# One token-block order and one early weight split in a fused decoder block on one core

## The chip, the cores and the metric

The kernel runs on one core of a Trainium2 chip. The metric is the device time in microseconds (us) of one execution of the whole program. The engines are TensorE (PE; its weight loads are PEld), VectorE (DVE), ScalarE (ACT), GpSimd (POOL) and SyncE (SP), which issues every DMA of this kernel from one in-order queue.

## The reference, cut to what matters

One decoder layer over 1024 tokens of width 1024, all in float32: a hybrid token mixer (convolution, stick-breaking attention, RWKV-7), cross-attention into 256 memory tokens, and a gated feed-forward part with a convolution. Each begins with an RMS norm, each is added to the stream, and a final norm follows.

```python
def rms_norm(x, g):
    y = x * lax.rsqrt(jnp.mean(x * x, axis=-1, keepdims=True) + RMS_EPS)
    return y * g

def conv_ffn(hn, w_up, conv_w, conv_b, w_down):      # w_up 1024 x 5632, w_down 2816 x 1024
    u = causal_dwconv(hn @ w_up, conv_w) + conv_b     # width 3, per channel, along tokens
    gate, val = jnp.split(u, 2, axis=-1)
    return (jax.nn.silu(gate) * val) @ w_down

h = h + mix                                           # token mixer, projected by w_mix_out
h = h + memory_cross_attention(rms_norm(h, norm_ca), rms_norm(mem, norm_mem), ca_wq, ca_wkv, ca_wo)
h = h + conv_ffn(rms_norm(h, norm_ffn), ffn_up, ffn_conv_w, ffn_conv_b, ffn_down)
return rms_norm(h, norm_final)
```

## The kernel before, in words

**Numbers.** Every float32 operand of a large product is split into a rounded part "hi" and a rest "lo" (ACT casts hi, then VectorE or POOL computes source minus hi). A product is three matmuls per contraction block: hi·hi, hi·lo, lo·hi, each 128 x 128 by 128 x 512.

**Stages.** The token mixer ends with a merge: activations mh and ml (pool "ma") are multiplied with rows of w_mix_out (pool "wm") and accumulated into the eight token tiles h0 to h7 (128 tokens x 1024). `accumulate` (L1070) does such a sum: for each token tile, all matmuls into a two-bank PSUM tile (pool pd, two buffers), then one VectorE addition into h[i] (L1088), or an ACT copy (L1091) where there is nothing to add to, then a callback `after(i)`. Then comes cross-attention: `norm_T` (L193) normalises the eight tiles, transposes them on TensorE and splits them into hh and hn_lo; `q_proj` makes the queries of a head (L245 to L247 for head 0, by halves of 512 tokens), `attend` the head's output, and an `accumulate` with rows of ca_wo adds it to h.

**Into the feed-forward part.** The last of these accumulations (L1316) has the callback `operands(i)`, tile after tile in the order 0 to 7: store h[i] to h_d, normalise (sum of squares on ACT L189, short one-column operations on VectorE L190 and L176 to L181, the multiply by rs and the gain at L1277, written into h[i] or h[i−6]), transpose (L1296), copy back into h (L1299), and `put` split operands into X (L1280: ACT cast, lo on POOL for t1, t3 and t4, on VectorE otherwise).

The up product uses a two-by-two block scheme with seven products instead of eight. Blocks are the halves of the model width and the even or odd token tiles. b11 and b21 come from even tiles alone; b22, t1, t2, t3 and t4 need an even tile and the odd one behind it (L1305 to L1314).

**Up.** For each of 22 tiles f (L1370): four raw weight blocks are loaded, sums of weights are made on POOL (`wsum` L1332), each of seven weights is split (`parts` L1339, L1340), and seven products of twelve matmuls follow in the order b11, b21, t2, t3, t4, t1, b22 (L1346 to L1348); VectorE adds them up (L1368), then come the convolution (L1360 to L1364), the Silu, the product on POOL (L1399) and the store to hid_d[f].

**Down.** hid_d[0] and row 0 of ffn_down are loaded, split (`pair`) and multiplied without an addition; then groups of 2, 2, 3, 3, 3, 4, 4 rows follow. The first group has the callback `residual` (POOL adds h_d back, L1417), the last `final` (norm and store).

**Order.** The program is written in program order with priorities (`tc.high_priority`); a scheduler puts the instructions of each engine in order by priority and by when it expects operands to be ready. Each engine then runs in order.

**Memory.** Pools are stacks, from the left or (side right) from the right end of SBUF; the size of a pool is the sum of its tiles, and a tile that takes the place of a closed pool's tile waits for the last reader of that tile (`reuse_waits="tile"`). In bytes per partition: constants end at 2432; the mixer's pools mconst, wf, ft, mg and ma follow each other from there, ma from 59776 (four mh of 4096) with its four ml from 76160 to 92544. Cross-attention then opens, from 2432 again, wc (18432: weights of wq), can (19456: gain, junk, four ss, rs and rt each, two xs), and after can is closed wo (20480), co (16384), cq and ca. hn_lo (on the right) lies over wm.

Of the kernel before, what the change touches and what calls it, by code (L numbers as in the profile page):

```python
# [15 lines left out]
P = 128  # L16
# [30 lines left out]
POOL_T = ("t1", "t3", "t4")  # L47
AHEAD_TILES = 2
# [3 lines left out]
def hybrid_block(tc, A, out):  # L52
# [30 lines left out]
    with root:  # L83
# [100 lines left out]
        def rms(pl, xt, junk=None):  # L184
# [6 lines left out]
            return rsqrt(pl, ss, 1)  # L191
# [939 lines left out]

        with ExitStack() as st:
            wp = pool(st, "wc", 2)
            s3 = ExitStack()
            hnp = pool(s3, "hn", side=RIGHT)
# [7 lines left out]
            wo = pool(st, "wo", 2)  # L1143
            op = pool(st, "co", 2)
# [126 lines left out]
            gb = bcast_row(np_, A["norm_ffn"][0:1, :], "gb")  # L1271

            def normed(i):
# [14 lines left out]
            def operands(i):  # L1288


                with tc.high_priority(offset=100):
                    xs = normed(i)
                for b in range(2):
                    ps = PQ()
                    for j in range(4):
                        pe.transpose(out=ps[:, j * P:(j + 1) * P],  # L1296
                                     in_=xs[:, (4 * b + j) * P:(4 * b + j + 1) * P],
                                     identity=ident)
                    s_.copy(half(i, b), ps.rearrange("p (j t) -> p j t", j=4))  # L1299
# [15 lines left out]

            accumulate(wo, o, wrows, after=operands, rbufs=2)  # L1316

        with fst as st:
            up = A["ffn_up"][0].rearrange("(k p) c -> p k c", p=P)
            wp = pool(st, "wu")  # L1320
            wpt = [wp.tile([P, 2, 4, P], F32R, name="wp", bufs=10)]

            def raw(kh, c):
                t = wp.tile([P, 4, P], F32, name="raw", bufs=6)
# [155 lines left out]
```

## Time and profile before

| | us |
|---|---|
| median of three runs | 2319.57 |
| lowest and highest run | 2318.44, 2321.55 |
| profiled execution | 2328.44 |
| its span, first to last instruction | 2326.7 |
| TensorE busy in it | 2218.7 (95%) |
| VectorE, ACT, POOL busy | 1459.3, 896.5, 571.2 |

The profile is of one execution, which was 8.9 us longer than the median of the runs. All positions are us from the start of its span. Matmuls overlap: one of 512 columns shows about 0.39 us and the next starts earlier, so rates are read from the distance between starts. A few matmul records are missing in any stretch.

### The profile page before, as it was taken

What the parts mean: (1) busy time and instruction counts of PE and PEld (TensorE: products, weight loads), DVE (VectorE), ACT (ScalarE), POOL (GpSimd) and SP (SyncE); (2) the same over time, 40 slices, a digit from 0 to 9 for tenths busy, and PEclk for the clock granted to TensorE, in tenths of its full rate; (3) what the DMA queues carried; (4) which work ended last, traced back from release to release, by engine and by line L of the source; (5) the groups of instructions that cost most, each with busy time, mean ns of one, the idle gap of its engine ahead of it and who ended that gap; (6) DMA issues with size and microseconds to landing.
All of it is one profiled execution on the core that took longest, in us unless ns stands there. A gap on an engine that the chain in (4) does not pass through costs nothing.

```text
span 2326.7 us, 29997 instructions
## 1 busy us (share of the span) xinstructions
PE 2218.7 (95%) x11635; PEld 1838.7 (79%) x11635; DVE 1459.3 (63%) x1994; ACT 896.5 (39%) x1494; POOL 571.2 (25%) x489
## 2 busy tenths in 40 slices
PE   6999999999999999999998999996899999989998
PEld 5888878878888888887877878884788888867886
DVE  7576555672254254356767675449988888867535
ACT  6644233433344244345431153225444444442212
POOL 1124322232232233221112000002544444413000
PEclk9999989998999999999999999997899999999999
DMA  4334624433211211214767121103222222155311
GB/s 156 120 111 157 209 77 133 143 87 92 73 48 52 82 64 53 84 55 150 231 208 259 57 60 32 32 28 109 73 82 82 82 82 82 67 179 185 108 33 73
DMA packets 230112, 237.89 MB, mean 102 GB/s; under 512 B 35283, under 2 KB 188113, under 8 KB 228945
## 3 DMA queue, kind: packets, MB, share of 16 engines
q1 hardware_dynamic: 229969, 235.97, 31.3%
q8 instruction: 91, 1.49, 0.3%
q14 instruction: 52, 0.43, 0.1%
HBM read 169.87 MB, written 66.06 MB: 101 GB/s over the span
## 4 chain that ended last, share of the span: by engine, by line
PE 77%; DVE 12%; DMA 3%; issue 3%; ACT 3%; POOL 1%; SPq 0%; DVEq 0%; ACTq 0%; POOLq 0%
PE pd L276 6%; PE pd L275 6%; PE pd L279 6%; PE pd L1082 5%; PE pd L1083 5%; PE pd L1086 5%; PE pd L1346 3%; PE pd L1348 3%; PE pd L1347 3%; PE pd L257 3%; PE pd L260 3%; PE pd L256 3%; PE pq L1346 2%; PE pq L1348 2%; PE pq L1347 2%
## 5 line engine op out<-in xcount | busy, mean ns | idle before, releaser
L235 ACT CAST wh<-wr 128x512 fp32r<-128x512 f32 x270 | 159.0, 621 | 364.5 <-PE pd L1086 105.6
L236 POOL TENSOR_TENSOR wl<-wr,wh 128x512 fp32r<-128x512 f32 x128 | 177.4, 1403 | 261.1 <-ACT wh L235 247.7
L275 PE MATMUL pd<-xn_hi,wh 128*128 128x512 f32 x576 | 227.7, 395 | 0.0
L1088 DVE TENSOR_TENSOR h<-pd,h 128x1024 f32<-128x1024 f32 x120 | 146.5, 1221 | 126.8 <-PE pd L1086 126.5
L276 PE MATMUL pd<-xn_lo,wh 128*128 128x512 f32 x576 | 225.1, 391 | 0.0
L279 PE MATMUL pd<-xn_hi,wl 128*128 128x512 f32 x576 | 178.4, 391 | 0.0
L256 PE MATMUL pd<-xn_hi,wh 128*128 128x512 f32 x384 | 152.8, 398 | 0.0
L257 PE MATMUL pd<-xn_lo,wh 128*128 128x512 f32 x384 | 152.3, 397 | 0.0
L236 DVE TENSOR_TENSOR wl<-wr,wh 128x512 fp32r<-128x512 f32 x142 | 105.9, 768 | 60.8 <-ACT wh L235 60.5
L929 DVE TENSOR_TENSOR_SCAN B<-B 128x128 f32<-128x128 f32 (+3 forms) x64 | 87.0, 1359 | 85.1 <-POOL B L926 84.8
L279 PEld LDWEIGHTS pd<-xn_hi,wl 128*128 128x128 f32 x576 | 108.0, 188 | 23.6 <-POOL wl L236 0.2
L276 PEld LDWEIGHTS pd<-xn_lo,wh 128*128 128x128 f32 x576 | 108.4, 188 | 19.8
L275 PEld LDWEIGHTS pd<-xn_hi,wh 128*128 128x128 f32 x576 | 108.2, 188 | 19.5
L260 PE MATMUL pd<-xn_hi,wl 128*128 128x512 f32 x384 | 122.9, 398 | 0.0
L1340 DVE TENSOR_TENSOR wp<-ws,wp 128x512 fp32r<-128x512 f32 x88 | 121.0, 1375 | 2.4 <-ACT wp L1339 1.8
L1399 POOL TENSOR_TENSOR h<-h,h 128x1024 f32<-128x1024 f32 x22 | 52.8, 2402 | 227.5 <-DVE h L1364 192.7
L946 DVE TENSOR_TENSOR al<-pq,ah 128x512 fp32r<-128x512 f32 x80 | 54.6, 688 | 85.7 <-ACT ah L945 85.2
L1346 PE MATMUL pq<-t,wp 128*128 128x512 f32 x264 | 102.8, 389 | 2.5 <-ACT wp L1339 2.5
L1339 ACT CAST wp<-ws 128x512 fp32r<-128x512 f32 x88 | 54.7, 622 | 128.5 <-POOL ws L1332 66.0
L1347 PE MATMUL pq<-t,wp 128*128 128x512 f32 x264 | 102.9, 390 | 0.0
L1348 PE MATMUL pq<-t,wp 128*128 128x512 f32 x264 | 102.7, 389 | 0.0
L945 ACT CAST ah<-pq 128x512 fp32r<-128x512 f32 x80 | 46.9, 587 | 144.7 <-PE pq L941 144.4
(395 smaller groups left out, 5807.0 us busy)
## 6 DMA issues: line engine op xcount, KB each, us to landing
wr<-in_w_comb_dram SPq DMA_DIRECT2D x124, 256.0 KB
raw<-in_ffn_up_dram SPq DMA_DIRECT2D x88, 256.0 KB
gate_d<-ft SPq DMA_DIRECT2D x24, 512.0 KB
hid_d<-h SPq DMA_DIRECT2D x22, 512.0 KB
wr<-in_ffn_down_dram SPq DMA_DIRECT2D x42, 256.0 KB
t<-hid_d SPq DMA_DIRECT2D x21, 512.0 KB
wr<-in_ca_wkv_dram SPq DMA_DIRECT2D x32, 256.0 KB
ft<-gate_d SPq DMA_DIRECT2D x16, 512.0 KB
```

The source lines that it names most:

```text
L235: s_.copy(hi[:, sl], raw)
L236: (v_ if lo_e == "dve" else g_).tensor_tensor(lo[:, sl], raw, f32(hi[:, sl]), ALU.subtract)
L256: pe.matmul(o, wh(k), xh(k, h), start=k == 0, stop=False)
L257: pe.matmul(o, wh(k), xl(k, h), start=False, stop=False)
L260: pe.matmul(o, wl(k), xh(k, h), start=False, stop=k == nk - 1)
L275: pe.matmul(o, wh(k), xh(k, h), start=k == 0, stop=False)
L276: pe.matmul(o, wh(k), xl(k, h), start=False, stop=False)
L279: pe.matmul(o, wl(k), xh(k, h), start=False, stop=k == nk - 1)
L1088: v_.tensor_tensor(h[i], ps, h[i], ALU.add)
L1346: pe.matmul(ps, wh[:, k, :], xh[:, k, :], start=k == 0, stop=False)
L1347: pe.matmul(ps, wh[:, k, :], xl[:, k, :], start=False, stop=False)
L1348: pe.matmul(ps, wl[:, k, :], xh[:, k, :], start=False, stop=k == 3)
```

## The change

- The last attention accumulation takes the token tiles in the order 0, 2, 4, 6, 1, 3, 5, 7. Its callback `after` normalises tile i at once, and `operands` of an even tile follows once more than two tiles are waiting; odd ones come behind the accumulation.
- The weights of b11 and b21 for f = 0 and 1 are loaded and split ahead of this accumulation (`early_parts`, in a new pool "early"), and these four products stand between `operands` of the odd tiles.
- The normalised tile gets its own buffer xs (three) instead of a place in h. For even tiles POOL multiplies by the gain and ACT by rs; for odd ones VectorE does both, as before.
- `operands` reads the transposed tile from PSUM for splits and subtractions where it read a copy in h; odd tiles have only their first half copied.
- `rms` has its own short chain, with one VectorE operation less.
- wo and co are opened before wc, behind "early"; wc moves into the stack that closes with the queries.
- At f = 14, hid_d[0] and row 0 of ffn_down are loaded and split into the "early" tiles (`early_pair`), and the down part begins with them in the order 4, 0, 1, 5, 3, 7, 6, 2. The first group's two weight rows and activations go into the top tile by `pair`.

```diff
@@ rms
-            return rsqrt(pl, ss, 1)
+            r = pl.tile([P, 1], F32, name="rs", bufs=4)
+            t = pl.tile([P, 1], F32, name="rt", bufs=4)
+            s_.activation(t, ss, AF.Sqrt)
+            v_.reciprocal(r, t)
+            v_.scalar_tensor_tensor(t, r, ss, r, ALU.mult, ALU.mult)
+            v_.tensor_scalar(t, t, -0.5, 1.5, ALU.mult, ALU.add)
+            v_.tensor_tensor(r, r, t, ALU.mult)
+            return r
@@ cross-attention
+        est = ExitStack()
+        early = pool(est, "early")
         with ExitStack() as st:
-            wp = pool(st, "wc", 2)
+            wo = pool(st, "wo", 2)
+            op = pool(st, "co", 2)
             s3 = ExitStack()
+            wp = pool(s3, "wc", 2)
...
-            wo = pool(st, "wo", 2)
-            op = pool(st, "co", 2)
             ap = pool(s3, "cq", 2)
@@ into the feed-forward part
+            def early_parts(kh, c):
+                t = early.tile([P, 4, P], F32, name="er")
+                dma(t, up[:, 4 * kh:4 * kh + 4, c * P:(c + 1) * P])
+                w = early.tile([P, 2, 4, P], F32R, name="ew", bufs=4)
+                s_.copy(w[:, 0], t)
+                g_.tensor_tensor(w[:, 1], t, f32(w[:, 0]), ALU.subtract)
+                return w[:, 0], w[:, 1]
+
+            first = [[early_parts(kh, f) for kh in range(2)] for f in range(2)]
...
-                rs = rms(np_, h[i])
-                xs = h[i] if i < 6 else h[i - 6]
-                v_.scalar_tensor_tensor(xs, h[i], rs, gb, ALU.mult, ALU.mult)
+                xs = np_.tile([P, D], F32, name="xs", bufs=3)
+                if i % 2 == 0:
+                    g_.tensor_tensor(xs, h[i], gb, ALU.mult)
+                    s_.activation(xs, xs, AF.Copy, scale=rms(np_, h[i]))
+                else:
+                    v_.scalar_tensor_tensor(xs, h[i], rms(np_, h[i]), gb, ALU.mult, ALU.mult)
...
-            def operands(i):
+            def operands(i, xs):
                 q = i // 2
+                p1, p2 = turned(xs, 0), turned(xs, 1)
                 if i % 2 == 0:
-                    put("b11", half(i, 0), q)
-                    put("b21", half(i, 1), q)
+                    for b, (n, ps) in enumerate((("b11", p1), ("b21", p2))):
+                        put(n, ps, q)
+                        s_.copy(half(i, b), ps)
                     return
                 b11, b21, b12, b22 = half(i - 1, 0), half(i - 1, 1), half(i, 0), half(i, 1)
-                put("b22", b22, q)
+                s_.copy(b12, p1)
                 v_.tensor_tensor(b11, b12, b11, ALU.subtract)
                 put("t1", b11, q)
-                v_.tensor_tensor(b12, b22, b12, ALU.subtract)
+                v_.tensor_tensor(b12, p2, b12, ALU.subtract)
                 put("t3", b12, q)
-                v_.tensor_tensor(b22, b22, b11, ALU.subtract)
+                v_.tensor_tensor(b22, p2, b11, ALU.subtract)
+                put("b22", p2, q)
                 put("t2", b22, q)
...
-            accumulate(wo, o, wrows, after=operands, rbufs=2)
+            todo = []
+            def after(i):
+                with tc.high_priority(offset=100):
+                    todo.append((i, normed(i)))
+                if len(todo) > LAG and todo[0][0] % 2 == 0:
+                    operands(*todo.pop(0))
+            accumulate(wo, o, wrows, after=after, rbufs=2, order=(0, 2, 4, 6, 1, 3, 5, 7))
+            done = []
+            for f in range(2):
+                done.append(even_products(*first[f]))
+                for _ in range(1 + f):
+                    operands(*todo.pop(0))
+            operands(*todo.pop(0))
+            for f in range(2):
+                even_sums(f, *done[f])
@@ up
+                if f >= 2:
+                    even_sums(f, *even_products(parts(a11), parts(a12)))
...
+                if f == EARLY_DOWN:
+                    d0 = early_pair(hid_d[0]), early_pair(down[0])
@@ down
-            accumulate(None, [pair(d0, h[0], hid_d[0], "a")], [pair(d0, h[4], down[0], "w")],
-                       add=False, order=(2, 6, 0, 4, 1, 5, 3, 7))
...
+                if gi == 0:
+                    ws = [pair(None, hp2.tile([P, T], F32, name="t", bufs=3), down[k], x[1])
+                          for k, x in zip(ks, tiles[2:])]
+                    accumulate(None, [d0[0]], [d0[1]], add=False, order=(4, 0, 1, 5, 3, 7, 6, 2))
+                    gbf = bcast_row(hp2, A["norm_final"][None, :], "gbf")
+                    accumulate(None, acts, ws, after=residual)
```

`even_products` issues the products of b11 and b21 into one pd tile, `even_sums` copies and adds them; `early_pair` loads a row in two halves through the one er tile, casts on ACT and subtracts on POOL. LAG is 2, EARLY_DOWN is 14.

## Rows read from the trace of the kernel before

**Rows 1.** The page, engine totals: busy us, share of the span, instructions.
```profile
PE 2218.7 (95%) x11635; PEld 1838.7 (79%) x11635; DVE 1459.3 (63%) x1994; ACT 896.5 (39%) x1494; POOL 571.2 (25%) x489
```
**Rows 2.** Windows: us, busy us of each engine (instructions), granted clock, DMA share, GB/s.
```profile
1353.30:1385.10 31.80, 30.00 (x151) 23.47 (x152) 25.12 (x48) 14.61 (x27) 0.00 (x0) 1.00 0.30 88
1610.00:1620.00 10.00, 1.94 (x8) 1.57 (x8) 10.00 (x14) 5.56 (x12) 6.17 (x5) 0.50 0.08 32
1660.00:2060.00 400.00, 400.00 (x1750) 326.52 (x1750) 345.35 (x367) 167.01 (x225) 178.06 (x98) 1.00 0.25 80
```
**Rows 3.** Waits of TensorE, 1500 to 1660: who for whom, us, times, longest.
```profile
PE pq L1296 <- DVE h L1277: 12.6, 2, 7.6
PE pq L1296 <- DVE ss L190: 6.2, 2, 4.3
```
**Rows 4.** Waits of TensorE, 2040 to the end.
```profile
PE pd L1082 <- ACT h L1091: 3.5, 2, 2.8
PE pd L1082 <- DVE h L1088: 3.3, 2, 2.6
PE pd L1083 <- DVE wl L1429: 1.8, 1, 1.8
```
**Rows 5.** Timeline of TensorE, several stretches: start, us, line, operands, [idle before].
```profile
1384.86 0.39 PE L247 MATMUL pd<-top,wl 128*128 128x512 f32 x1
...
1574.43 0.73 PE L1082 MATMUL pd<-wh,oh 128*128 128x512 f32 x2 [1.92 <-ACT wh L235]
...
1637.36 0.40 PE L1348 MATMUL pd<-top,wp 128*128 128x512 f32 x1
1640.26 0.50 PE L1346 MATMUL pq<-t,wp 128*128 128x512 f32 x1 [2.50 <-ACT wp L1339]
...
2062.47 0.39 PE L1348 MATMUL pd<-b,wp 128*128 128x512 f32 x1
...
2063.15 0.39 PE L1348 MATMUL pd<-b,wp 128*128 128x512 f32 x1
...
2317.15 0.61 PE L1086 MATMUL pd<-wh,al 128*128 128x512 f32 x2
```
**Rows 6.** VectorE by line, 1577 to 1640: busy us, mean ns, idle before.
```profile
L1277 DVE SCALAR_TENSOR_TENSOR h<-h,rs,gb 128x1024 f32<-128x1024 f32 x8 | 13.8, 1740 | 0.0
L1088 DVE TENSOR_TENSOR h<-pd,h 128x1024 f32<-128x1024 f32 x8 | 9.7, 1218 | 3.6 <-PE pd L1086 3.5
...
L1311 DVE TENSOR_TENSOR h<-h,h 128x512 f32<-128x512 f32 x4 | 4.8, 1205 | 0.0
...
L178 DVE TENSOR_TENSOR rt<-rs 128x1 f32<-128x1 f32 x8 | 3.3, 426 | 0.0
...
L1309 DVE TENSOR_TENSOR h<-h 128x512 f32<-128x512 f32 x4 | 2.7, 681 | 0.2 <-ACT h L1299 0.2
L179 DVE TENSOR_TENSOR rt<-rt,ss 128x1 f32<-128x1 f32 x8 | 2.2, 290 | 0.0
```
**Rows 7.** The page's costliest groups: busy us, mean ns, idle before.
```profile
L236 POOL TENSOR_TENSOR wl<-wr,wh 128x512 fp32r<-128x512 f32 x128 | 177.4, 1403 | 261.1 <-ACT wh L235 247.7
...
L1340 DVE TENSOR_TENSOR wp<-ws,wp 128x512 fp32r<-128x512 f32 x88 | 121.0, 1375 | 2.4 <-ACT wp L1339 1.8
L1399 POOL TENSOR_TENSOR h<-h,h 128x1024 f32<-128x1024 f32 x22 | 52.8, 2402 | 227.5 <-DVE h L1364 192.7
```
**Rows 8.** Timeline of VectorE, cross-attention's norm.
```profile
1336.30 0.16 DVE L177 RECIPROCAL rs<-rt 128x1 f32<-128x1 f32 x1
...
1337.27 1.28 DVE L210 SCALAR_TENSOR_TENSOR xs<-h,rs,gb 128x1024 f32<-128x1024 f32 x1
...
1353.47 4.94 DVE L222 TENSOR_TENSOR hn_lo<-pq,top 128x512 fp32r<-128x512 f32 x8
...
1372.89 1.29 DVE L222 TENSOR_TENSOR hn_lo<-pq,top 128x512 fp32r<-128x512 f32 x2 [0.23 <-ACT top L221]
```
**Rows 9.** Timeline of ACT, the first Square of that norm.
```profile
1333.61 1.06 ACT L189 ACTIVATE junk<-h 128x1024 f32<-128x1024 f32 x1 [9.43 <-DVE h L1088]
```

More of the change, by code (lines that the diff above doesn't have):

```diff
@@ L1357, in q3, with plus, places, even_products @@
                 return ps.rearrange("p (q t) -> p q t", t=P)
+            def plus(o, ps, x):
+                v_.tensor_tensor(o, q3(ps), q3(x), ALU.add)
+            def places(f):
+                e = f % 2
+                return h[2 * e], h[4 + 2 * e], h[2 * e + 1], h[5 + 2 * e]
+            def even_products(w11, w12):
+                ab = PD()
+                return product(ab[:, 0:512], w11, "b11"), product(ab[:, 512:1024], w12, "b21")
+            def even_sums(f, pa, pb):
+                t0, t1, u0, u1 = places(f)
+                s_.copy(t0[:, 0:512], pa)
+                plus(blocks(u0)[0], pb, t0[:, 0:512])
@@ new lines, in hybrid_block, with early_pair, raw, wsum @@
+            operands(*todo.pop(0))
+            for f in range(2):
+                even_sums(f, *done[f])
+        with fst as st:
+            wp = pool(st, "wu")
+            down = [A["ffn_down"][0, k * P:(k + 1) * P, :] for k in range(NF)]
+            def early_pair(src):
+                ws = [early.tile([P, 2, 4, P], F32R, name="ew", bufs=4)
+                      .rearrange("p x a t -> p (x a t)") for _ in range(2)]
+                for sl in (slice(0, 512), slice(512, 1024)):
+                    t = early.tile([P, 4, P], F32, name="er").rearrange("p a t -> p (a t)")
+                    dma(t, src[:, sl])
+                    s_.copy(ws[0][:, sl], t)
+                    g_.tensor_tensor(ws[1][:, sl], t, f32(ws[0][:, sl]), ALU.subtract)
+                return ws
+            def raw(kh, c):
+                t = wp.tile([P, 4, P], F32, name="raw", bufs=6)
+                with tc.high_priority(offset=400):
+                    dma(t, up[:, 4 * kh:4 * kh + 4, c * P:(c + 1) * P])
+                return t
+            def wsum(x, y, op):
+                t = wp.tile([P, 4, P], F32, name="ws", bufs=3)
+                with tc.high_priority(offset=ahead):
+                    g_.tensor_tensor(t, x, y, op)
+                return t
+            def parts(src):
+                t = wp.tile([P, 2, 4, P], F32R, name="wp", bufs=10)
+                hi, lo = t[:, 0], t[:, 1]
+                with tc.high_priority(offset=ahead):
+                    s_.copy(hi, src)
+                    v_.tensor_tensor(lo, src, f32(hi), ALU.subtract)
+                return hi, lo
@@ L1365, in conv @@
                                         ALU.mult, ALU.add)
[L1367 to L1368 removed]
             for f in range(NF):
[L1371 removed]
                 ahead = 0 if f < AHEAD_TILES else 100
[L1373 removed]
+                t0, t1, u0, u1 = places(f)
                 (u0e, u0o), (u1e, u1o) = blocks(u0), blocks(u1)
@@ L1430, in pair, with hidden @@
                 return hi, lo
[L1432 to L1443 removed]
+            def hidden(ks, tiles):
+                return [pair(x[0], hp2.tile([P, T], F32, name="t", bufs=3), hid_d[k], x[1])
+                        for k, x in zip(ks, tiles)]
             f = 1
```

68 lines of the change are left out of this document (17 added, 51 removed).

## Prediction

> **What bounds the kernel now.** TensorE is busy for 95% of the span [rows 1], so only stretches in which it waits or runs slowly can be won. I read the page first, then ten-microsecond windows, then the waits of TensorE in the two thin stretches. The first lies where cross-attention hands over to the feed-forward part: in 1610 to 1620 TensorE is busy for 1.94 us of 10 while VectorE is full, and the granted clock is 0.50, the lower of its two levels [rows 2]. TensorE's transposes wait there for the normalisation on VectorE, 12.6 and 6.2 us [rows 3]. The second lies where the down products begin [rows 4].
>
> How much is there? A 512-column matmul comes every 0.227 us (three from 2062.47 to 2063.15 [rows 5]). From 1574.43, the start of the last attention accumulation, to 2063.38, the end of the up products, 489.0 us pass. They hold 96 + 1848 matmuls, 440.7 us, and 64 transposes, 7.7 us by an estimate of 0.12 each. So 40.6 us are lost. From 2063.38 to 2317.76, the end of the last matmul, 254.4 us hold 1056 matmuls, 239.4: 15.0 lost, of which 8.6 are the three waits of [rows 4]. No edit here can win more than about 55 us.
>
> **Into the feed-forward part: 18 us won.** VectorE sets this stretch. What the change takes from it, by [rows 6]: four of the eight normalising multiplies (even tiles go to POOL and ACT), half of 13.8, 6.9 us; the subtraction behind b22 now reads PSUM, so its four go from 1.205 to the 0.681 of the line above it that already did (4.8 to 2.7), 2.1; the two short operations of L178 and L179 become one, 5.5 less about 3.0, so 2.5. Together 11.5 us. The first matmul that needs odd tiles (product t2) then starts at 1640.26 − 11.5 = 1628.8 [rows 5]. By then TensorE has done 48 up matmuls instead of the 12 done now (one product, ended at 1637.8 [rows 5]), as both even tiles' products of f = 0 and 1 lie beside odd transposes: 36 × 0.227 = 8.2 us more. That cover costs TensorE nothing, since it idled there. Against it, VectorE needs 345.35 / 400 × 19.05 = 16.4 us per up tile [rows 2], and f = 0 and 1 now have only 60 matmuls, 13.6 us, for 16.4 − 2 × 1.375 [rows 7] = 13.7 us of it: I take 2 us of stall. 11.5 + 8.2 − 2 = 18 (17.7). The low end is 6.5, should the VectorE saving vanish; the high end 30, as most of 40.6 needs both operands and weights, which stay behind the last h_d stores in SP's queue. The four early weight loads are moved ahead of those eight stores; their ACT casts and POOL subtractions (4 × 1.40 by the POOL line of [rows 7]) lie before 1585, where POOL is empty; without that cover they would cost POOL 5.6 us.
>
> What is late next is POOL: four h·gb multiplies of 2.40 us (L1399's form [rows 7]) join it, with the odd tiles' t-parts queued behind them.
>
> *The port.* An operation of the kind of L1277 took 1.28 us with POOL idle [rows 8] and 1.74 on average here; L1088, with one input in PSUM, kept 1.218 [rows 6]. The Trainium skill, SBUF — State Buffer, "Who interferes with whom", says that a VectorE instruction with two SBUF inputs and a GpSimd one that reads SBUF lock each other out for a whole instruction. The rows agree. By that rule the four multiplies put on POOL could hold VectorE for 4 × 2.40 = 9.6 us, and the gain here would be 8 instead of 18; this is rival two.
>
> **Into the down products: 10 us won.** hid 0 and down row 0 are loaded and split at f = 14, so the wait for the split weights (1.8) goes, and the one for copies that stood among casts on ACT (3.5) shrinks, with what the clock loses between them. The order 4, 0, 1, 5 first writes tiles that f = 21 does not use; tiles 6 and 2 still wait for its last multiply and store, 1 to 4 us. Most of the 3.3 us of waits for additions stays, as POOL still adds eight residuals beside VectorE's splits. So 15.0 − 5 = 10, between 4 and 14. The early pair adds 4 SP loads through one buffer (three of them held until POOL is done with the one before, with up-weight loads queued behind), 4 ACT casts and 5.6 us of POOL. POOL is busy for 178 of 400 us there [rows 2], which hides them; if the weight queue runs dry, up to 5. I take 0.5 lost.
>
> **One operation less in each rsqrt of one column: 1 us won** in the first 50 us, where TensorE waits on that chain, and 0.2 at the end; between 0 and 2.
>
> **What moves without being meant to: 14.5 us lost.** Pools are stacks, so places follow from tile sizes. Now wc lies at 2432 and the cross-attention norm's pool "can" at 20864 (bytes per partition), over tiles long dead. After the change early (18 KB), wo (20 KB) and co (16 KB) come first, so wc starts at 57728 and can covers 76160 to 95616. The merge's eight activation buffers ("ma") end at 92544 and their low parts start at 76160. Whichever two of the four the last accumulation reads, its readers are on the place of can's junk, ss or xs, until its last matmul. That such a wait binds is seen now: hn_lo lies over this accumulation's weights, and its first eight subtractions come in one block at 1353.47 [rows 8], though the first xs was ready at 1338.5. So the first Square, at 1333.61 now [rows 9], must wait until about 1353.3. Behind it on ACT wait the casts of wq, whose buffers wh lie over the same tiles; on SP the wq loads, then the mk and mv loads; on VectorE the short chain.
>
> Price: the first xs came 3.66 us after its Square (1333.61 to 1337.27), so at 1357.0. From there VectorE has 8 × 1.28 (xs), 16 × 0.62 (4.94 / 8), 7 × 0.97 less one operation (L177 to L210 in [rows 8]), say 6.5, and 4 × 0.65 of weights: 29.2 us, to 1386.2. Now the last hn_lo starts at 1372.89 and ends at 1374.2. TensorE needs the last token tile for the second halves of both first q tiles, 48 matmuls, 10.9 us: 1397.1 against 1385.1 now (the last L247 [rows 5]), 12.0 lost. If it keeps the written order, 72 are left, 16.3, and 17.4 lost. I take 14.5, between them. The low end is −2: the wait is not there, and the 1.8 us go in which TensorE is idle between 1353.3 and 1385.1 now [rows 2]. The high end is 36: the whole overlap, 19.7, plus 5.4 for the order, plus 48 matmuls at half clock, 10.9. TensorE is saturated afterwards, so nothing gives this back.
>
> **Sum.** −18 − 10 − 1 + 0.5 + 14.5 = −14 us. The profiled execution took 2328.4 us (span 2326.7 and 1.7 around it), 8.9 above the median of the runs; it would become 2314.4, and the median 2319.6 − 14 = 2305.6.
>
> **Rivals.**
> 1. The norm's wait costs nothing. For: the places hold only if the pools are laid as I read them. Against: hn_lo's block. Gain 28.5: 2291.
> 2. POOL's new multiplies stretch VectorE until its 11.5 us are gone. For: L1277's 1.74 and the 0.43 of a one-column operation in L178 [rows 6]. Against: even tiles' other work mostly has an input in PSUM. Then 6.5 + 10 + 1 − 0.5 − 14.5 = 2.5 won: 2317.
> 3. Slower: the norm's wait takes the place of the stall that is removed. It sits before the first q product; all eight norm tiles, their transposes and the wq casts run after 1353.3, one behind another, with TensorE at the lower clock. From 28.5 us on, the sum of all gains, it decides; at its high end of 36 the time is 2327. For: VectorE has 29 us there with nothing to run beside. Against: TensorE has 10.9 us of first halves to fill in.
> 4. The change doesn't do what it says: the even products come after the odd operands because the order of instructions is chosen by priority and readiness. Then 8.2 is lost: 2314. It lies in my own range.
>
> **How the numbers follow.** My forecast, with rival 4 in it, 0.62, its own range 2295 to 2316. Rival 1 0.15, rival 2 0.13, rival 3 0.10. About 0.2%, 4.6 us, can be told from no change: under 2315 is faster, over 2324.2 slower. Faster: nearly all of 0.62 (0.59), 0.15 and a third of rival 2 (0.04), 0.78. Same: 0.03 and the rest of rival 2, 0.12. Slower: 0.10. The range goes from 2286 (rival 1 with a little more) to 2318.
>
> **What would show it.** In the profile after: the norm's first Square about 20 us later against the merge's last matmul, a hole in TensorE of 10 to 18 us before the first q products, and the last L247's counterpart 12 to 17 us later. Twelve-matmul products for f = 0 and 1 among the odd transposes, the first t2 product 54 us after the start of the accumulation before it instead of 66; VectorE's normalising line with four entries. The down products with at most 5 us of waits in their first 60 us. I am wrong if the q products start as early as now, if t2 waits for weights on SP or POOL instead of operands, or if up tiles 0 to 3 lose more than 5 us on VectorE.

## The result, and the profile after

The changed kernel takes 2348.57 us (median of 4 runs, 2346.20 to 2352.59) against 2320.56 us for the kernel before (4 runs): ratio 1.0122, 95% interval 1.0105 to 1.0140. It is 28 us slower; the forecast was 2305.6, 15 us faster. The forecast was wrong in its sign.

Three marks of TensorE's timeline cut the profiled executions into stages: the end of the merge's last matmul, the start of the last attention accumulation (as in the prediction, the seventh of its 96 matmuls, behind its wait for the second row's weights), and the end of the up products. An end is a row's start plus its length, here and below (the prediction took 0.1 to 0.2 us less).

| stage, us | before | after | difference | forecast |
|---|---|---|---|---|
| span's start to merge's last matmul | 1353.3 | 1345.2 | -8.1 | -1 |
| to the start of the last attention accumulation | 221.2 | 238.0 | +16.8 | +14.5 |
| to the end of the up products | 489.1 | 490.8 | +1.7 | -17.5 |
| to the last matmul | 254.2 | 265.1 | +10.9 | -10 |
| to the span's end | 8.9 | 8.6 | -0.3 | -0.2 |

The sum is 21.0, the difference of the two profiled spans (2347.7 and 2326.7). The first row is no gain of the change: the profiled execution of before lay 8 us above its median, and its excess sits there. In the fifteen experiments whose code up to the merge is that of the change, that row lay between 1336.6 and 1351.5; in r1, with the code of before, it was 1353.3 in an execution 8 us above its median. The short chain, which works in every norm of this stage, didn't lower the median when tried alone (rms_only).

First, TensorE's marks after (timeline: start, us, line, operands, [idle before <- what ended it]); they answer to [rows 5].

```profile
1344.62 0.61 PE L1095 MATMUL pd<-wh,ml 128*128 128x512 f32 x2
1351.34 3.43 PE L225 MATMUL pq<-ident,xs 128*128 128x128 f32 x16 [6.10 <-DVE ss L192]
...
1583.22 1.22 PE L1091 MATMUL pd<-wh,oh 128*128 128x512 f32 x2 [1.77 <-ACT wh L244]
...
1649.38 0.79 PE L1346 MATMUL pq<-t,wp 128*128 128x512 f32 x1 [16.50 <-ACT wp L1427]
...
2073.66 0.39 PE L1348 MATMUL pd<-b,wp 128*128 128x512 f32 x1
```

Read the brackets. After the merge TensorE waits for VectorE's one-column operation on ss. Right before t2, the first product that needs odd tiles, it now waits 16.5 us at a stretch, for t2's weights (wp); before, it waited 2.5 us here [rows 5] and, ahead of that, for the normalisation [rows 3]. The prediction had named a wait for weights as a sign that it is wrong.

Second, the norm of cross-attention on ACT, which answers to [rows 9]:

```profile
1345.27 1.06 ACT L191 ACTIVATE junk<-h 128x1024 f32<-128x1024 f32 x1 [27.52 <-PE pd L1095]
```

The first Square starts 0.04 us after the merge's last matmul; before, it started 19.7 us ahead of it. This is the wait that the forecast read from the pools' places. The first q product starts 17.1 us after the merge (3.9 before), TensorE having been idle for 10.8 us of them, and the last q product of the first head ends 15.2 us later than before, counted from the merge: the three signs that the prediction named for this stage.

Third, VectorE by line from 1583 to 1645 (busy us, mean ns, idle before), to be held against [rows 6]:

```profile
L197 DVE SCALAR_TENSOR_TENSOR rt<-rs,ss 128x1 f32<-128x1 f32 x8 | 7.3, 935 | 0.1
L1303 DVE SCALAR_TENSOR_TENSOR xs<-h,rs,gb 128x1024 f32<-128x1024 f32 x4 | 6.6, 1646 | 0.0
```

The normalising multiplies did fall from 13.8 to 6.6 us, and the four subtractions behind b22 from 4.8 to 2.7, as forecast. But the one short operation that took the place of L178 and L179 costs 7.3 us where the two cost 5.5, and 3.0 was forecast. One of the eight, and what POOL did beside it (timeline):

```profile
1598.70 2.39 POOL L1300 TENSOR_TENSOR xs<-h,gb 128x1024 f32<-128x1024 f32 x1 [2.93 <-PE pq L1317]
1598.78 2.33 DVE L197 SCALAR_TENSOR_TENSOR rt<-rs,ss 128x1 f32<-128x1 f32 x1
```

Fourth, the end of POOL's queue before t2 (timeline):

```profile
1640.73 4.16 POOL L1309 TENSOR_TENSOR t<-h,t 128x512 fp32r<-128x512 f32 x3 [0.73 <-ACT t L1308]
1644.85 1.25 POOL L1340 TENSOR_TENSOR h<-h,h 128x512 f32<-128x512 f32 x1
1646.07 1.26 POOL L1420 TENSOR_TENSOR ws<-raw 128x512 f32<-128x512 f32 x1
1647.41 1.26 POOL L1420 TENSOR_TENSOR ws<-ws,raw 128x512 f32<-128x512 f32 x1
```

t2's weight is the second sum (x2, from 1647.41); it stands behind the odd tiles' t-parts. VectorE ended the operands at about 1643.8, 60.5 us after the accumulation's start (64.0 before): 3.5 us won, not 11.5.

Fifth, TensorE's waits from 2066 to the end (who for whom: us, times, longest), which answer to [rows 4]; there they were 8.6 in all, here 17.9.

```profile
PE pd L1091 <- ACT h L1100: 9.3, 4, 6.6
PE pd L1091 <- DVE h L1097: 8.6, 4, 5.0
```

### The profile page after: what moved, and what is told of

It is laid out like the page before. It is cut to its first block, busy times and chain, and to the rows that moved or that the text cites. A ratio compares the mean times of both kernels' runs of the same rounds, so it can differ in the third digit from the quotient of the medians.

```text
span 2347.7 us, 30015 instructions
## 1 busy us (share of the span) xinstructions
PE 2213.9 (94%) x11635; PEld 1839.8 (78%) x11635; DVE 1443.4 (61%) x1948; ACT 896.5 (38%) x1494; POOL 593.6 (25%) x501
## 5 line engine op out<-in xcount | busy, mean ns | idle before, releaser
L1097 DVE TENSOR_TENSOR h<-pd,h 128x1024 f32<-128x1024 f32 x120 | 146.3, 1222 | 149.9 <-PE pd L1095 149.8
L1428 DVE TENSOR_TENSOR wp<-ws,wp 128x512 fp32r<-128x512 f32 x88 | 119.8, 1362 | 13.9 <-ACT wp L1427 13.3
L1346 PE MATMUL pq<-t,wp 128*128 128x512 f32 x264 | 103.8, 393 | 16.5 <-ACT wp L1427 16.5
```

Source lines behind the costliest of these rows:

```text
L1097: v_.tensor_tensor(h[i], ps, h[i], ALU.add)
L1346: pe.matmul(ps, wh[:, k, :], xh[:, k, :], start=k == 0, stop=False)
```

## The experiments

The numbers, from each kernel's runs and its profile (stages as above; t2 from the last accumulation's start). Each ratio is to the runs of before on the same chip, with its 95% interval.

| kernel | median us | ratio | merge to last accumulation | to t2 | up part | down part |
|---|---|---|---|---|---|---|
| before | 2320.56 | | 221.2 | 65.8 | 489.1 | 254.2 |
| after | 2348.57 | 1.0122 (1.0105 to 1.0140) | 238.0 | 66.2 | 490.8 | 265.1 |
| e1_place | 2344.93 | 1.0102 (1.0083 to 1.0121) | 236.6 | 65.5 | 490.8 | 265.7 |
| e2_down | 2332.93 | 1.0048 (1.0033 to 1.0063) | 237.5 | 66.2 | 484.6 | 256.7 |
| e3_ahead0 | 2350.12 | 1.0116 (1.0096 to 1.0136) | 237.1 | 62.7 | 486.8 | 265.4 |
| rms_only | 2325.76 | 1.0013 (1.0000 to 1.0027) | 222.2 | 63.7 | 491.1 | 254.2 |
| e5_low | 2341.79 | 1.0087 (1.0069 to 1.0104) | 228.0 | 66.4 | 491.0 | 265.5 |
| e6_can | 2343.86 | 1.0101 (1.0082 to 1.0121) | 236.4 | 65.7 | 490.9 | 265.3 |
| e7_can | 2336.39 | 1.0071 (1.0050 to 1.0092) | 225.8 | 63.0 | 486.8 | 264.9 |
| c1 | 2327.12 | 1.0023 (1.0013 to 1.0034) | 228.6 | 66.4 | 484.7 | 254.5 |
| c1_vec | 2320.87 | 0.9996 (0.9983 to 1.0008) | 229.2 | 61.5 | 480.5 | 254.9 |
| c4 | 2315.32 | 0.9977 (0.9966 to 0.9988) | 226.6 | 60.0 | 479.1 | 254.7 |
| c5 | 2316.61 | 0.9975 (0.9963 to 0.9987) | 226.5 | 59.8 | 479.8 | 254.9 |
| c6 | 2317.57 | 0.9984 (0.9973 to 0.9995) | 221.8 | 61.4 | 482.1 | 255.3 |
| d1 | 2330.52 | 1.0035 (1.0018 to 1.0051) | 226.3 | 60.2 | 485.7 | 263.9 |
| d2 | 2332.13 | 1.0048 (1.0035 to 1.0061) | 226.7 | 60.1 | 485.8 | 262.5 |
| p1 | 2320.45 | 0.9990 (0.9978 to 1.0002) | 227.1 | 62.9 | 482.2 | 254.8 |
| r1 | 2310.51 | 0.9954 (0.9940 to 0.9967) | 223.5 | 58.9 | 478.5 | 253.0 |

### Cross-attention: the place of the norm

**e1_place**

```diff
-            wp = pool(s3, "wc", 2)
             hnp = pool(s3, "hn", side=RIGHT)
+            pool(s3, "gap", side=RIGHT).tile([P, 512], F32, name="gap")
+            wp = pool(s3, "wc", 2, side=RIGHT)
-                np_ = pool(s2, "can", 1)
+                np_ = pool(s2, "can", 1, side=RIGHT)
```

> The changed kernel, but the pools of the cross-attention weights (wc) and of its norm (can) are put on the right side, at 110464 and 91008 bytes per partition, where neither lies over a tile that the merge's last accumulation reads. Theory: the norm waited for the merge because of its place alone. Then the norm's first Square comes about 20 us before the merge's last matmul, as in the kernel before, the stretch from the merge's last matmul to the last attention accumulation goes from 238.0 back to about 222, and the time from 2348.6 to about 2333. Rival: the norm is late because the scheduler ranks it behind the merge or because of VectorE; then the stretch stays at 235 to 240 and the time at 2347 to 2350.

The first Square did come 18 us before the merge's end (1326.82), yet the stage stayed at 236.6. VectorE's timeline in e1 shows why:

```profile
1344.60 1.23 DVE L1097 TENSOR_TENSOR h<-pd,h 128x1024 f32<-128x1024 f32 x1 [1.49 <-PE pd L1095]
1345.74 0.20 DVE L192 TENSOR_SCALAR ss<-ss 128x1 f32<-128x1 f32 x2
```

The ss operation waits for nothing but its turn: the sum of squares that it needs was there by 1330.8, and it stands in VectorE's queue behind all of the merge's additions (L1097). In the kernel before it stood among them.

**e6_can** and **e7_can** (can alone. The edit is e7's; in e6 the gap was e1's, so can lay at 109440 to 128896, not at the place that its expectation names, its upper 4 KB over wm)

```diff
+                pool(s2, "gap", side=RIGHT).tile([P, 1536], F32, name="gap")
-                np_ = pool(s2, "can", 1)
+                np_ = pool(s2, "can", 1, side=RIGHT)
```

> The changed kernel with the norm's pool can alone moved, to the right side at 105344 to 124800 bytes per partition, over neither ma nor wm; wc stays over ma, and wo, co and early stay as in the changed kernel. Theory: the norm's place costs most of the 16.9 us; the wq casts, which still wait for the merge, cost a few. Then the stretch is 223 to 230 and the time 2334 to 2341. Rival: the wq casts behind the merge cost as much by themselves: 232 to 238.

> The changed kernel with the norm's pool can alone at 105344 to 124800 bytes per partition, over no slot of ma or wm; wc stays over ma, wo, co and early stay. With it VectorE's one-column operations stand among the merge's additions again. Theory: any shared slot, even one that the last accumulation doesn't read, had put the norm behind the merge in VectorE's queue; without one the norm runs beside it, and what is left are the wq casts, which wait for the merge: the stretch to the last attention accumulation goes from 238.0 to 226 to 231, the time from 2348.6 to 2337 to 2342. Rival: the wq loads and casts alone keep the q products as late: 234 to 238 and 2345 to 2349.

e6 was again an e1: 236.4. e7, clear of every slot of ma and wm, brought the stage to 225.8 and the time down by 12 us. Its VectorE timeline:

```profile
1326.34 0.15 DVE L192 TENSOR_SCALAR ss<-ss 128x1 f32<-128x1 f32 x1 [1.22 <-ACT junk L191]
1326.62 1.22 DVE L1097 TENSOR_TENSOR h<-pd,h 128x1024 f32<-128x1024 f32 x1
```

So the norm's place costs 12.2 of the 16.8, with all else as in the change, and it acts through the order written into the queue: in e6 none of the norm's first operations waits for a matmul, so nothing that the last accumulation still reads lies under them, and yet the shared place was enough to put the norm behind the merge. The other 4.6 lie in e7 in the first head's q products, the last of which ends 36.9 us after the merge (32.0 before).

**e5_low**

```diff
-early = pool(est, "early")
+early = pool(est, "early", side=RIGHT)
...
+            # hn, can and the norm first; then
             wo = pool(st, "wo", 2)
             op = pool(st, "co", 2)
+            wp = pool(s3, "wc", 2)
```

> The changed kernel with other places for the cross-attention pools: the norm's pool can at 2432 and the weights' wc at 39296 bytes per partition, early on the right side, so that no tile of the norm or of wq lies over the merge's pools ma and wm, not even over slots that its last accumulation doesn't read. In e1 the Squares did come 18 us early, but VectorE's one-column operations still stood in its queue behind all of the merge's additions, as in the changed kernel; here they stand among them. Theory, sharpened: the place counts through the order of VectorE's queue, which is written for the tiles a pool lies over. Then the stretch from the merge's last matmul to the last attention accumulation goes from 238.0 to about 222 and the time from 2348.6 to about 2333. Rival: the late q products come from the weights wo and the early tiles, which now go through SP, ACT and VectorE first; here that is changed too, so only the next run tells.

228.0, not 222. The first q products come 3.9 us after the merge, as before, but then the tiles thin out. ACT in e5:

```profile
1357.09 0.62 ACT L1289 CAST ew<-er 128x512 fp32r<-128x512 f32 x1 [2.04 <-DMA er<-in_ffn_up_dram]
1357.62 1.07 ACT L230 CAST top<-pq 128x512 fp32r<-128x512 f32 x2
...
1362.14 0.62 ACT L1289 CAST ew<-er 128x512 fp32r<-128x512 f32 x1 [2.93 <-DMA er<-in_ffn_up_dram]
```

The casts of the early feed-forward weights, in their new place, wait for loads ahead of the norm's copies. That is a cost of this experiment's layout, taken up in c4.

### The down part and the early pair

**e2_down**

```diff
-                if f == EARLY_DOWN:
-                    d0 = early_pair(hid_d[0]), early_pair(down[0])
+            accumulate(None, [pair(d0, h[1], hid_d[0], "a")], [pair(d0, h[5], down[0], "w")],
+                       add=False, order=(4, 0, 1, 5, 3, 7, 6, 2))
...
```

> The changed kernel with the down part of the kernel before: no early pair at f = 14, the first pair is loaded and split when the up part ends (raws in h[1] and h[5], output order 4, 0, 1, 5, 3, 7, 6, 2), later groups in the old places. Theory: the down part's 10.9 us of loss come from the new start of the down part itself (the first products have no other work to cover the wait for f = 21's multiply and store, and the next groups' splits stand behind them). Then the last up product to the last matmul goes from 265.2 to about 255, the up part from 490.7 to about 490, and the time from 2348.6 to about 2338. Rival one: the down part is slow for a reason that stays (the order 4, 0, 1, 5 or h's new places): 263 to 266 and 2347 to 2349. Rival two: the early pair also stalls the up part (4 loads through one buffer): then the up part falls to 480 to 486 as well and the time is 2329 to 2334.

Both rival two and the theory: the down part came back to 256.7 and the up part fell to 484.6; 15.6 us in all. TensorE's waits in the up part after t2 show where the pair sat in it: 9.9 us in after, 5.2 here, and with the clock's loss 6.2. In program order the pair is at f = 14; the order by readiness drew its loads forward to f = 2 and 3 (they were issued from 1688.6 on).

**d1** and **d2** (d1 is c4, below, with the early pair, whose pool then stays open and whose old pool d0 is gone; d2 is d1 with the last store ranked first)

```diff
+                if f == EARLY_DOWN:
+                    d0 = early_pair(hid_d[0]), early_pair(down[0])
...
+                with tc.high_priority(offset=1000 if f == NF - 1 else 0):
-                dma(hid_d[f], t0)
+                    dma(hid_d[f], t0)
```

> c4 with the early pair of the change (hidden 0 and down row 0 split at f = 14 in program order) but the groups behind it as in the kernel before. Theory: the early pair is drawn forward to up tiles 2 and 3 by the scheduler and costs the up part 5 to 7 us there (480.5 to about 486); in the down part it saves the wait for the first split, 2 to 4 us (254.9 to 251 to 253), since the 8.4 us that e2 gave back in the down part came from the new groups. Net 2 to 4 us above c4. Rival: the down loss comes from the early pair itself (the first products start with nothing behind them ready): then the down part is 260 or more and the time 10 us above c4.

> d1 with one edit: the store of the last hidden tile ranks before the down weights' loads on SP. Theory: the early pair's loss in the down part is SP's order; the products into tile 2 wait for that store, issued 25.3 us after the last up product in d1 and 18.3 in c4. With the store at 19 to 20 the down part goes from 263.9 to 256 to 258, the time from 2330.5 to 2323 to 2325. Rival: it is the queue of ACT (the second convolution 11.4 us after the last up product in place of 2.5); then the down part stays at 261 to 264 and the time at 2328 to 2331.

The theory fell in d1: not the new groups but the early pair itself costs 9.2 us in the down part (254.7 to 263.9), and 6.6 in the up part. The chain that it meets is the last hidden tile's: convolutions on ACT and VectorE, Silu on ACT, product on POOL, store; a down product's copy into a tile that this chain still uses has to wait for it. From c4 (up products end at 2047.30):

```profile
2049.78 1.24 ACT L1416 ACTIVATE h<-h,prf 128x1024 f32<-128x1024 f32 x1
...
2063.20 2.36 POOL L1447 TENSOR_TENSOR h<-h,h 128x1024 f32<-128x1024 f32 x1 [25.43 <-ACT h L1445]
...
2065.59 1.01 ACT L1100 COPY h<-pd 128x1024 f32<-128x1024 f32 x1 [0.59 <-POOL h L1447]
```

and in the changed kernel (up products end at 2074.05):

```profile
2085.31 1.24 ACT L1432 ACTIVATE h<-h,prf 128x1024 f32<-128x1024 f32 x1
...
2089.81 5.54 POOL L1463 TENSOR_TENSOR h<-h,h 128x1024 f32<-128x1024 f32 x1 [25.30 <-DVE h L1436]
2090.28 1.01 ACT L1100 COPY h<-pd 128x1024 f32<-128x1024 f32 x1
2091.33 0.79 PE L1091 MATMUL pd<-ew 128*128 128x512 f32 x1 [6.61 <-ACT h L1100]
...
2095.39 1.01 ACT L1100 COPY h<-pd 128x1024 f32<-128x1024 f32 x1 [4.11 <-POOL h L1463]
...
2104.64 1.02 ACT L1100 COPY h<-pd 128x1024 f32<-128x1024 f32 x1 [0.69 <-DMA hid_d<-h]
```

Subtract the up products' end. In c4 both convolutions are on ACT by +2.5; here the second comes at +11.3, behind copies of the early products and casts. The product starts at +15.9 in c4, held by its Silu on ACT, and at +15.8 here, held by the second convolution's last step on VectorE (L1436): another gate, the same time, so starting the down products earlier didn't move it. Splits of later weights then run on VectorE beside the product, which takes 5.54 in place of 2.36 (3.20 in d1, 6.14 in d2), and the store goes out at +25.7 in place of +18.3.

Three copies of down products wait for this chain. The first needs the tile of that last step, which ends at +15.6: the copy comes at +16.2, though TensorE had ended its products at +10.7, and TensorE stands still for 6.6 us, its longest stop of the stage (7.8 in d1, at the same copy). The second waits for the product (+21.3; c4: +18.3), the third for the store (+30.6; c4: +22.1). d2 brought the store from +25.3 to +22.6, as early as its product allowed, and won 1.3 of the 9.2 in that stage, nothing in the median. So the store's place on SP is a small part. The longest stop hangs, by the profiles, on the second convolution's place in ACT's queue, which no run moves alone.

### Into the feed-forward part

**e3_ahead0**

```diff
-AHEAD_TILES = 2
+AHEAD_TILES = 0
```

> The changed kernel with AHEAD_TILES = 0, so that the weight sums and splits of up tiles 0 and 1 have the same early rank as those of later tiles. Theory: the first t2 product waits for its weights because POOL's sums stand behind the odd tiles' t-parts; ranked earlier, they are done before the operands and t2 starts when VectorE ends the last operand, about 60.5 us after the start of the last attention accumulation in place of 66.2; time 2342 to 2345. Rival: POOL is full in that stretch whatever the order, so what the sums gain the t-parts lose: t2 stays within 2 us of 66.2, time 2346 to 2351, or later where the sums push operands back.

The rival held: the median didn't move (six runs over 14 us). In the profile t2 came 3.5 us earlier and the up part was 4.0 shorter, but x1 still stood behind all but one of POOL's t-parts, and the operands themselves ended 3.3 us earlier (57.2 against 60.5). So the rank didn't do it; e7, which has the old rank, shows nearly the same, 62.9 and 486.8. In both, the L197 that took 2.33 beside POOL's fourth multiply in after ran clear of it in 0.22, and the next one met only its end (0.82 and 0.94).

**c1** (places of e5, down part of e2) and **c1_vec**

```diff
-                if i % 2 == 0:
-                    g_.tensor_tensor(xs, h[i], gb, ALU.mult)
-                    s_.activation(xs, xs, AF.Copy, scale=rms(np_, h[i]))
-                else:
-                    v_.scalar_tensor_tensor(xs, h[i], rms(np_, h[i]), gb, ALU.mult, ALU.mult)
+                v_.scalar_tensor_tensor(xs, h[i], rms(np_, h[i]), gb, ALU.mult, ALU.mult)
```

> The changed kernel with the down part of the kernel before (as in e2) and the places of e5: both are undone, the feed-forward entry with its even tiles first and early products stays. If the causes are separate they add: down 265 to 256, up part 490.8 to 484.6, cross-attention 238 to 222, so 2348.6 - 9 - 6 - 16 = about 2318 us. That would leave the entry itself at 4 us better than the kernel before. If one of them is given back elsewhere, 2324 or more.

> c1 with the even tiles normalised on VectorE as the odd ones are: no h*gb multiply on POOL, no scaling copy on ACT. Rival two of the forecast (POOL's multiplies hold VectorE at the shared port, seen in L197's 2.5 us beside them): the entry gains without them, t2 starts 2 to 5 us earlier than 66 after the last accumulation's start and the time is 2 to 5 us below c1. Theory: VectorE doesn't set t2's start, POOL's queue does (the odd tiles' t-parts, then x1 and x2); taking 4 x 2.4 us early out of POOL doesn't move the end of its queue, and VectorE has four more multiplies of 1.3 to 1.7: t2 0 to 5 us later, the time 0 to 5 us above c1.

c1's stages add as the single edits said (228.6, 484.7, 254.5); its median is 9 us above the 2318, of which 7 are e5's. c1_vec decided against the theory and for the forecast's rival two: giving VectorE four multiplies *more* made t2 4.9 us earlier and the kernel 6 us faster. VectorE's lines in c1, from 1576 to 1645:

```profile
L197 DVE SCALAR_TENSOR_TENSOR rt<-rs,ss 128x1 f32<-128x1 f32 x8 | 7.3, 936 | 0.1
L1303 DVE SCALAR_TENSOR_TENSOR xs<-h,rs,gb 128x1024 f32<-128x1024 f32 x4 | 6.6, 1644 | 0.0
```

and in c1_vec:

```profile
L1299 DVE SCALAR_TENSOR_TENSOR xs<-h,rs,gb 128x1024 f32<-128x1024 f32 x8 | 10.2, 1281 | 0.1
...
L197 DVE SCALAR_TENSOR_TENSOR rt<-rs,ss 128x1 f32<-128x1 f32 x8 | 1.6, 215 | 0.0
```

The eight short operations and four multiplies take 13.9 us with POOL beside them; the same eight and eight multiplies take 11.8 without. The edit also takes ACT's scaling copies away, which the next run keeps out.

**p1** (c4 with POOL's products put back, into a buffer that nothing reads)

```diff
+                if i % 2 == 0:
+                    for b in range(2):
+                        sl = slice(512 * b, 512 * b + 512)
+                        g_.tensor_tensor(early.tile([P, 4, P], F32, name="er")
+                                         .rearrange("p a t -> p (a t)"),
+                                         h[i][:, sl], gb[:, sl], ALU.mult)
```

> c4 with POOL multiplying h and gb for the even tiles as in the change (8 x 512 columns), into a buffer that nothing reads; VectorE still normalises all eight tiles, ACT makes no scaling copies. Theory: the port alone stretches VectorE: L197's one-column operations go from 0.2 to 0.6 to 1.0 each, the normalising multiplies from 1.28 to 1.5 to 1.7, together 5 to 7 us of VectorE, and t2 starts 3 to 5 us later than in c4 (60.0 to 63 to 65), time 3 to 5 us above c4. Rival: POOL's multiplies are over before its t-parts begin and VectorE has slack; then the one-column operations stretch but t2 stays at 60 to 61 and the time within 1 us of c4: what c1_vec won was then ACT's copies and the order.

The theory held in t2 and the time: t2 at 62.9 (60.0 in c4), the up part 3.1 us longer, the time 3 us above c4 by the two ratios (5 by the medians, from different chips). Nothing depends on these products and ACT has no more to do, so it is VectorE's stretching that costs. Its lines in p1, from 1560 to 1640:

```profile
L1305 DVE SCALAR_TENSOR_TENSOR xs<-h,rs,gb 128x1024 f32<-128x1024 f32 x8 | 11.2, 1414 | 0.1
...
L197 DVE SCALAR_TENSOR_TENSOR rt<-rs,ss 128x1 f32<-128x1 f32 x8 | 2.8, 364 | 0.0
```

They stretched by less than in c1 (0.364 against 0.936), with POOL's pieces half as long; in all by some 3 us over c4, where 5 to 7 were expected.

**c4**, **c5** and **c6** (on c1_vec: early weights after the last q projection; then t2's sums on VectorE; then no early products)

```diff
-        early = pool(est, "early", side=RIGHT)
...
+            early = pool(est, "early", side=RIGHT)
             fst = ExitStack()
```

> c1_vec with one edit: the pool early is opened after the last q projection, over hn_lo, so that the four early weights are loaded and split after cross-attention's norm and not among its tiles. In e5, c1 and c1_vec their casts stood on ACT waiting for their loads, 2.0, 2.9 and 2.2 us, ahead of the norm's copies, and their POOL subtractions stretched one-column operations of VectorE to 1.0 to 1.3 us. Theory: these make up the 7 us that the stretch from the merge to the last attention accumulation still has over the 221.2 of the kernel before; it goes from 229.2 to 221 to 223, and the time from 2320.9 to 2313 to 2315. Rival: the 7 us are wc's or wo's new places; then the stretch stays at 227 to 230 and the time at 2319 to 2322.

```diff
+                on = v_ if f == 0 else g_
-                x1 = wsum(a21, a22, ALU.add)
-                x2 = wsum(x1, a11, ALU.subtract)
+                x1 = wsum(a21, a22, ALU.add, on)
+                x2 = wsum(x1, a11, ALU.subtract, on)
```

> c4 with the two weight sums of up tile 0 that t2 waits for (x1 and x2) on VectorE in place of POOL. Theory: in c1_vec VectorE ends the last operand at 57.3 us after the last accumulation's start, and t2 starts at 61.5, since POOL reaches x2 only then, in its queue behind the odd tiles' t-parts; so t2 starts at 58 to 60 and the time is 1 to 4 us below c4. Rival: the sums delay operands on VectorE by as much (two operations of 0.7 to 1.2), so t2 stays at 61 to 62 and the time is that of c4.

```diff
-                if f >= 2:
-                    even_sums(f, *even_products(parts(a11), parts(a12)))
+                even_sums(f, *even_products(parts(a11), parts(a12)))
```

> c4 without the early products: no early weights, and the even products of up tiles 0 and 1 come where those of other tiles do; the token order and the operand chain stay. The forecast put 36 matmuls more beside the odd transposes at 8.2 us. Theory: the 48 early products do lie in time in which TensorE would idle, so without them the up part from the last accumulation's start gets 7 to 11 us longer (480.5 to 488 to 492). Rival: what is won there is lost again, since up tiles 0 and 1 then have too few matmuls to cover VectorE and POOL: 481 to 485.

c4: the time fell by 5.5 us, nearly the 6 to 8 of the theory, but the stage only from 229.2 to 226.6. c6 accounts for the rest: without the early weights it is 221.8, nearly the 221.2 of before. In c4 they stand among the last softmaxes, where TensorE waits 2.3 us once for VectorE's e. c5: no gain, as its rival said; VectorE takes the two sums after the last operand, at 1.75 and 1.63 us beside POOL's t-parts. c6: the early products are worth 3.0 us (479.1 to 482.1), not 8.2, and their weights cost 4.8 one stage earlier; the two kernels are equal within their intervals.

### The short chain

**rms_only** (before with the short chain) and **r1** (c4 with the long one)

```diff
-            return rsqrt(pl, ss, 1)
+            v_.scalar_tensor_tensor(t, r, ss, r, ALU.mult, ALU.mult)
+            ...
```

> The kernel before with one edit of the change alone: the shortened chain of one-column operations in rms. Theory of the forecast: 1 us faster, 2319 to 2320. Rival: the 8 us by which the merge's last matmul came earlier in the changed kernel (1345.2 against 1353.3) are this edit's: then 2311 to 2314, and the merge ends at about 1345 here. If it ends there and the time stays at 2319, the kernel before's profile was simply a slow one upstream of the merge.

> c4 with the longer chain of one-column operations in rms, as in the kernel before. Forecast: 1 us slower than c4, most of it in the first 50 us. Rival, from rms_only's ratio of 1.0013: the short chain with its operation that reads three one-column operands costs 2 to 3 us somewhere upstream, so this is 2312 to 2313.

Both forecasts missed, and both runs point the same way: the short chain adds 3 us to before (at the edge of its interval) and taking it out of c4 wins 5 (0.9954 against 0.9977; the intervals touch). One operation less is not a gain here. In the profiles r1 is 3.1, 0.6 and 1.7 us shorter in the three stages; but the order of many instructions moves with this edit, and the stage up to the merge, where most of the chains are, can't be read from single profiles. Why the short chain costs stays open.

r1, 0.46% faster than the kernel before, is the best version. Of the change it keeps the even tiles first, their early products, the buffers xs, VectorE's subtractions from PSUM and the down part's order of tiles; the rest is undone, and the pools lie as in c4.

## Why the prediction was wrong

**What moves without being meant to: 14.5 us lost.** Right in sign, place and size: 16.8. The first Square stood where it was forecast, and the price was worked out from a norm that runs whole behind the merge, which it did. But the reason was only half of it: e1 took the wait on the last readers away and won 1.4 us, since the places also decide the order in VectorE's queue. That the size fits is in part luck. Order and wait together, taken away in e7 for the norm alone, cost 12.2 us; the remaining 4.6 sit in the first head's q products and agree with wq's casts, which still come behind the merge there, but no run moves these alone. (The early weights aren't in it: in e7 they are split before the merge ends, from 1297.6 on; the 4.8 that c6 measures are for their place in c4.)

**Into the feed-forward part: 18 us won.** Failed: 1.7 lost. Four terms of its sum failed.
- The VectorE saving of 11.5. Moving four multiplies to POOL was taken as 6.9 won, with VectorE's other operations at their old length; by c1 and c1_vec it lost 4.2 us of the up part (with ACT's copies; 3.1 by p1 for POOL's products alone). The "two short operations" that "become one", 2.5 won, became 1.8 lost. How much is lost hangs on where a multiply falls: in the profiles of e3 and e7 the operands ended 57.2 and 57.3 us after the accumulation's start, as in c1_vec (57.3), and not at 60.5 (after) or 60.8 (c1). Rival two had this mechanism, with the port at a chance of 0.13 and no more than the saving at stake; beside POOL the whole gain and more was lost. Here the Trainium skill, SBUF — State Buffer, "Who interferes with whom", was right where the sum went by the rows: a VectorE instruction with two SBUF inputs and a GpSimd one that reads SBUF lock each other out for a whole instruction. The trace agrees: L197, 0.21 alone, took 2.33 in a row of after beside a POOL multiply of 2.39.
- The 8.2 for the even products: 3.0, by c6.
- "What is late next is POOL", said and given no price. It set t2: x2's sum was ready 5 us after the operands, whose 3.5 us gained so came to nothing.
- The early pair, 0.5 lost: 6.2 by e2, 6.6 by d1, since it was drawn forward to the tiles that have no slack.

The 40.6 us that the prediction counts as lost in this stretch are 42.0, as 90 and not 96 matmuls of the accumulation lie behind its mark; nothing hangs on it. What is left of the entry is real: c4's up part is 10.0 us shorter than before. 489.1 − 10.0 + 4.2 (POOL's multiplies) + 6.2 (the early pair) is 489.5, against 490.8 measured.

**Into the down products: 10 us won.** Failed: 10.9 lost. The step "the wait for the split weights goes" was right and worth nothing: by "tiles 6 and 2 still wait for its last multiply and store, 1 to 4 us" the forecast named the gate, but took it as fixed, and left out the tile that the second convolution still uses. The early start put work of the down part in front of that gate: on ACT (the second convolution, 8.8 us later than in c4), on VectorE (splits beside POOL's product, 3.2 us) and on SP. TensorE's longest stop, 6.6 us, waits for the convolution, by the profile; that it is the early pair which brings all this is shown by d1, how the 9.2 us divide is not.

**One operation less in each rsqrt: 1 us won.** Not seen; the runs say 3 to 5 lost.

**The rivals.** The slower side was there (rival three, 0.10) but by a single mechanism at its high end. What came is the sum of three: the norm's late start about as priced, rival two at more than its price, and the early pair, which the forecast counted as a gain.

## What to carry to other kernels

Work that is moved ahead of a gate is worth only what lies behind the gate: ask what the last chain before it (here convolution, POOL's product, copy, store) shares with the work that is now let in front of it, on every queue. An operation moved from VectorE to POOL has to be priced with what it does to VectorE's operations beside it, the shortest with two SBUF inputs above all. And after any change of pools read the order of the queues next to the places: a tile over a slot of a pool in use can put a whole chain behind that pool's stage.

## What the runs showed of the hardware

A one-column operation of VectorE that reads two SBUF inputs and meets a POOL operation on SBUF ends only when that one ends: 0.21 alone, 0.88 beside a piece of 512 columns in p1, 2.33 beside 1024 in after. VectorE's one-input operations (0.14, L192 at 1590.29 in after) and its additions from PSUM (1.22, L1097) kept their length beside the same multiplies. It goes the other way as well: POOL's 1024-column product, 2.36 alone, took 5.54 in after and 6.14 in d2, where VectorE's splits went on without a gap for 3.3 and 3.9 us from its start; the product's own 2.2 us came behind them. The granted clock followed TensorE's holes: 0.63 from 1640 to 1660 and 0.71 from 2080 to 2100 in after, between its two levels, TensorE being busy for 10.6 and 11.0 of 20 us there. Behind the 16.5 us hole the matmuls started 0.43 us apart at first (1651.09, 1651.52, 1651.95), where they later start every 0.227; so a hole cost more than its length.
